# A one-layer decoder step on one core: feature tiles 4 and 5 as a stage of their own, and elementwise work in a fixed order by weight quarter

## The chip, the core and the metric

The kernel runs on one core of a Trainium2 chip. The time is the device time of that core from the start to the end of one execution, in microseconds (us). TensorE is called PE in the rows of the profile, and its weight loads PEld; VectorE is DVE, ScalarE is ACT, GpSimd is POOL, and SyncE, which issues the transfers, is SP.

## The reference, cut to what matters

One layer computes, for 256 prompt tokens and 8 x 4 sample tokens together (288 columns):

```
mod = silu(c) @ w_ada + b_ada            # six modulation vectors
h   = rms(x, g_mix) * (1 + sc_m) + sh_m
...                                      # two mixers, merged
x   = x + gt_m * (merged @ w_out)
h2  = rms(x, g_ffn) * (1 + sc_f) + sh_f
gate, up = split(h2 @ w_ffn_in)          # 2048 -> 2 x 5632
x   = x + gt_f * ((silu(gate) * up) @ w_ffn_out)
y   = rms(x, g_final)
```

The change touches the start of the FFN: the line that makes `h2` and the first columns of `h2 @ w_ffn_in`.

## The kernel before

Everything is held with features on the 128 partitions and tokens along the free axis: `x` is 16 feature tiles of 128 x 288. A product of a weight tile (128 x 128) and an activation tile (128 x 288) is made with three matmuls: both operands are split into a rounded high part and the rest, the low part, and high x high, high x low and low x high are added in PSUM (lines 501 to 503). So every weight tile that arrives costs two elementwise instructions besides the matmuls: ACT casts it to `hi`, DVE subtracts to `lo`. They are made for four 128 x 128 tiles at a time, 128 x 512 elements, called a quarter here, since a 1 MB block of weights has four of them. `Blk.high` and `Blk.low` make one quarter. Four `hi` and four `lo` buffers turn (`SPB = 4`), so a quarter's cast waits until PE is through with the quarter four before it.

The stream of weights is read in blocks of 1 MB by transfers on SP, five blocks ahead (`RAW = 5`). The main loop at the end of `_body` walks through `steps`: it issues the load of the block five steps on, splits blocks up to one ahead of the one that runs, and runs the step. A step of class `Do` is a piece of elementwise work. Where the wrapper `Pinned` has `on` set, the instructions of VectorE or ScalarE keep the order in which the code names them; with `on = None`, as from the `wD` blocks on, the scheduler may place them by its own priorities.

The output columns of `w_ffn_in` are grouped in 128-wide feature tiles, gate and up in turn: tiles 0 and 1 are the first gate and its up, 2 and 3 the second. The first four tiles are the stage `fk`. Their product needs `h2`, which needs the sum of squares of the whole finished `x`. To have PE busy meanwhile, `fk` multiplies the unnormalised `xg = x * gm2` (`scaled`, 298 columns: 288 tokens and the nine shift vectors and one of zeros), k by k, four output tiles side by side in four PSUM banks; `sink_fk` multiplies by the row factor `rb2` and adds the shift afterwards. Four blocks of four k each, each k with 12 matmuls.

Between these matmuls the row factor is made. `rstd2` runs behind matmul group (1, 1) of the first block: DVE adds the last square to the accumulator (`acc<-acc,t`), PE sums over partitions with a column of ones (three matmuls `px<-ones,acc`), DVE scales (`r<-px`), POOL takes the power -1/2 (`r<-r,mhalf`). `norm2` behind group (2, 2) spreads it: three matmuls `px<-ident,r`, an ACT copy `rb<-px`. Then `modulate` makes the 16 tiles of `h2`, in three pieces between the blocks of `fk`: for each k a DVE product `s<-x,rb`, an ACT affine step `t<-s,mod,gm`, two small POOL steps for the sample columns, an ACT cast `s<-t` (high part) and a DVE subtraction `s<-t,s` (low part).

Behind `fk` come the blocks `fi`, one feature tile each with all 16 k one after another (48 matmuls of 288 columns), from tile 4 on. A quarter of such a block holds four k. The 18 tiles 4 to 21 are woven with 16 steps of the last modulation product (`a5`), then the rest of the FFN follows in four parts. At the end of block 3 of `fk` all four of its PSUM banks are drained by `sink_fk` at once; `sink_fi` then joins gate and up.

Of the kernel before, what the change touches and what calls it, by code (L numbers as in the profile page):

```python
# [57 lines left out]
    "fk": (0, 4, 4),  # L58
    "fi": (0, 16, 1),
# [21 lines left out]
def _body(tc, nc, d, pc, pw, pslot, ptmp, pps):  # L81
# [150 lines left out]
    def turn(t, n=T):  # L232
        return t[:, :n].rearrange("p (a b) -> p b a", a=2)
# [308 lines left out]
    class KBlk(Blk):  # L542
        def run(self):
            if self.idx == 0:
                S["kps"] = [psmain() if j else psmisc() for j in range(self.nm)]
            nb = 16 // self.nk
            for k in range(self.nk):
                ah, al = (turn(t, TU) for t in self.rhs(self.idx * self.nk + k))
                first, last = self.idx + k == 0, self.idx == nb - 1 and k == self.nk - 1
                for j in range(self.nm):  # L550
                    ps = S["kps"][j]
                    wh, wl = self.parts[k * self.nm + j]
                    PE.matmul(ps[:, :TU], wh, ah, start=first, stop=False)  # L553
                    PE.matmul(ps[:, :TU], wh, al, start=False, stop=False)  # L554
                    self.last = PE.matmul(ps[:, :TU], wl, ah, start=False, stop=last)  # L555
                    for f in self.then.get((k, j), ()):
                        f()
            if self.idx == nb - 1:
                for j, ps in enumerate(S.pop("kps")):
                    self.sink(j, ps)  # L560
# [326 lines left out]
    def mk_h2(k0, k1):  # L887
        def f():
            modulate(range(k0, k1), lambda k: normed(k, S["rb2"]), gm2, 48, h2)

        return Do(f)


    act = {}

    def sink_fi(i, ps):
        f, up = i // 2, i % 2
        if not up:
            S["gate"] = ps
            return  # L900
        pg = S.pop("gate")
# [254 lines left out]
    def ffin(q):  # L1156
        fi = [Blk("fi", i - 4, h2.__getitem__, lambda j, ps: sink_fi(j + 4, ps)) for i in range(max(4, 22 * q), 22 * q + 22)]
        return fi
# [4 lines left out]
    fk = [KBlk("fk", i, xg.__getitem__, sink_fk) for i in range(4)]  # L1163
    fk[0].defer = fk[1].defer = True
    fk[0].then = {(1, 1): [rstd2], (2, 2): [norm2]}
    steps += [Do(fk[0].split), fk[0], Do(lambda: fk[1].split()), mk_h2(0, 6), fk[1], mk_h2(6, 11), fk[2], mk_h2(11, 16), fk[3]]
    a5 = ada("a5")
    steps += weave(ffin(0), [eight(a5[:8]), eight(a5[8:])], 0, 17)
# [175 lines left out]
```

## Time and profile before

| | us |
|---|---|
| runs shown | 1523.9, 1524.02, 1525.62 (median 1524.02) |
| the profiled execution, device time | 1523.81 |
| span of its instructions | 1521.9 |
| PE busy (share of the span) | 1511.2 (99%) |
| DVE busy | 994.1 (65%) |
| ACT busy | 742.4 (49%) |
| POOL busy | 135.4 (9%) |

The profiled execution is 0.2 us under the median; some 1.9 us of it lie before the first and after the last instruction. A row of the timeline has the start in us from the start of the span, the duration, engine, source line, operation, what is written and read, shapes, and in brackets how long the engine had been idle and what ended that. Matmuls are pipelined: one lasts 0.29 us, and the next starts 0.12 us after it; so a stall of PE is read from the distance of two starts, and seldom shows as idle time.

### The profile page before, as it was taken

Reading aid. Unit: us, or ns where it says so; the run is one execution under the profiler, and the core shown is the slowest. Engines: PE = TensorE matmul, PEld = TensorE weight load, DVE = VectorE, ACT = ScalarE, POOL = GpSimd, SP = SyncE. Lnnn points to the kernel's source line nnn. Section 1 sums busy time; section 2 is a strip of 40 time slices with the busy share of each in tenths; the row PEclk is TensorE's granted clock in tenths of the full one; section 3 lists DMA queues with packets and bytes.
Section 4 is the critical chain, followed back from the end, with each engine's and each line's share of the span. In section 5 each row is a group of like instructions: output and inputs, shape, how many; then the busy total and the mean of one; then the engine's idle time right before and its main releaser. Section 6 shows DMA issues by size and latency. Waiting matters only on the chain.

```text
span 1521.9 us, 31756 instructions
## 1 busy us (share of the span) xinstructions
PE 1511.2 (99%) x12596; PEld 1447.6 (95%) x12596; DVE 994.1 (65%) x2003; ACT 742.4 (49%) x1375; POOL 135.4 (9%) x272
## 2 busy tenths in 40 slices
PE   9999999999999999999999999999999999999997
PEld 7898999999899998989999899999999999999997
DVE  5886778978756666657954466555665556655575
ACT  5443454744445444447744444444444444444465
POOL 2554410000100000012300000000000000000000
PEclk9999999999999999999999999999999999999999
DMA  9877875777877788775599656554565545655452
GB/s 378 342 288 300 355 267 188 278 272 281 299 298 291 287 274 306 258 260 176 173 311 337 218 180 223 169 191 135 180 215 189 170 159 167 218 176 179 141 182 88
DMA packets 74436, 357.70 MB, mean 235 GB/s; under 512 B 8384, under 2 KB 28640, under 8 KB 44080
## 3 DMA queue, kind: packets, MB, share of 16 engines
q1 hardware_dynamic: 73792, 354.88, 65.6%
q8 instruction: 98, 1.61, 0.4%
q0 software_dynamic: 352, 0.73, 0.1%
q14 instruction: 50, 0.41, 0.1%
q10 hardware_dynamic: 144, 0.07, 0.0%
HBM read 352.56 MB, written 3.09 MB: 234 GB/s over the span
## 4 chain that ended last, share of the span: by engine, by line
PE 98%; DMA 1%; ACT 0%; DVE 0%; issue 0%; SPq 0%; DVEq 0%; POOL 0%; POOLq 0%
PE pm L501 30%; PE pm L503 30%; PE pm L502 30%; PE ada L383 6%; PE px L267 1%; DMA raw<-in_aB 1%; DMA raw<-in_aA 0%; PE pm L553 0%; PE pm L554 0%; PE pm L555 0%; PE pm L537 0%; PE px L595 0%; PE pm L267 0%; PE px L553 0%; PE px L554 0%; PE px L555 0%
## 5 line engine op out<-in xcount | busy, mean ns | idle before, releaser
L501 PE MATMUL pm<-s,hi 128*128 128x288 f32 (+1 forms) x3704 | 1063.3, 287 | 0.1
L503 PE MATMUL pm<-s,lo 128*128 128x288 f32 (+1 forms) x3704 | 1059.7, 286 | 0.2 <-DVE lo L115 0.2
L502 PE MATMUL pm<-s,hi 128*128 128x288 f32 (+1 forms) x3704 | 1059.5, 286 | 0.0
L115 DVE TENSOR_TENSOR lo<-raw,hi 128x512 fp32r<-128x512 f32 (+2 forms) x967 | 667.3, 693 | 404.3 <-ACT hi L115 390.6
L115 ACT CAST hi<-raw 128x512 fp32r<-128x512 f32 (+2 forms) x964 | 583.1, 606 | 663.3 <-PE pm L502 590.8
L501 PEld LDWEIGHTS pm<-s,hi 128*128 128x128 f32 x3704 | 700.0, 189 | 12.3 <-issue 10.2
L503 PEld LDWEIGHTS pm<-s,lo 128*128 128x128 f32 x3704 | 700.1, 189 | 0.4 <-DVE lo L115 0.4
L502 PEld LDWEIGHTS pm<-s,hi 128*128 128x128 f32 x3704 | 700.1, 189 | 0.0
L383 PE MATMUL ada<-raw,cs 128*32 128x512 f32 (+3 forms) x768 | 75.3, 525 | 1.7 <-DMA raw<-in_aB 0.9
L976 POOL TENSOR_TENSOR r<-r,mhalf 128x3 f32<-128x3 f32 x1 | 0.9, 863 | 768.4 <-DVE r L115 768.4
L115 DVE TENSOR_TENSOR s<-pm,s 128x288 f32<-128x288 f32 x128 | 57.5, 454 | 16.9 <-PE pm L503 16.5
L115 ACT CAST s<-t 128x288 fp32r<-128x288 f32 (+2 forms) x109 | 50.5, 465 | 24.1 <-DVE t L115 21.9
L383 PEld LDWEIGHTS ada<-raw,cs 128*32 128x32 f32 x768 | 21.7, 109 | 36.7 <-issue 27.4
L115 DVE TENSOR_TENSOR s<-t,s 128x288 fp32r<-128x288 f32 (+1 forms) x109 | 50.3, 463 | 7.9 <-ACT s L115 7.5
L115 DVE SCALAR_TENSOR_TENSOR t<-t,pm 128x288 f32<-128x288 f32 x84 | 37.9, 451 | 11.2 <-PE pm L503 11.2
L115 DVE SCALAR_TENSOR_TENSOR x<-pm,mod,x 128x256 f32<-128x256 f32 (+1 forms) x81 | 38.2, 472 | 2.4 <-PE pm L503 2.4
L278 POOL TENSOR_TENSOR t<-x,gm 128x32 f32<-128x32 f32 x16 | 7.9, 491 | 250.3 <-DVE acc L115 237.9
L665 POOL TENSOR_TENSOR s<-s,rb 128x288 f32<-128x288 f32 x30 | 29.6, 1009 | 0.0
L115 DVE SCALAR_TENSOR_TENSOR s<-pm,s 128x288 f32<-128x288 f32 x48 | 24.3, 510 | 0.0
L115 ACT ACTIVATE t<-x 128x288 f32<-128x288 f32 (+2 forms) x32 | 13.7, 428 | 19.2 <-DVE x L115 19.2
L666 POOL TENSOR_TENSOR s<-s 128x32 f32<-128x32 f32 x48 | 22.6, 484 | 0.0
L115 DVE TENSOR_TENSOR acc<-acc,t 128x288 f32<-128x288 f32 x36 | 16.4, 455 | 8.7 <-ACT t L115 8.7
(147 smaller groups left out, 558.5 us busy)
## 6 DMA issues: line engine op xcount, KB each, us to landing
raw<-in_fi SPq DMA_DIRECT2D x84, 1024.0 KB, 4.9
raw<-in_a SPq DMA_DIRECT2D x48, 1024.0 KB, 4.9
raw<-in_f SPq DMA_DIRECT2D x64, 704.0 KB, 4.1
raw<-in_wD SPq DMA_DIRECT2D x36, 1024.0 KB, 8.5
raw<-in_wC SPq DMA_DIRECT2D x20, 896.0 KB, 6.4
raw<-in_aE SPq DMA_DIRECT2D x16, 1024.0 KB, 6.8
s<-in_a SPq DMA_DIRECT2D x128, 128.0 KB, 5.3
raw<-in_wo SPq DMA_DIRECT2D x16, 1024.0 KB, 6.1
```

Of the source, the lines that this page charges most:

```text
L115: i = f(*args, **kw)
L267: return in_order(op(*args, **kw))
L278: G.tensor_tensor(sam(a[:, TP:T]), sam(x[:, k, TP:]), bc4(gm[:, k, 1:]), ALU.mult)
L383: PE.matmul(acc[32 * j : 32 * j + 32, c], cs[:, kt, :], self.raw[2 * j + h] if self.apart else self.raw[:, o : o + w], start=(kt < ks), st ...
L501: PE.matmul(ps[:, : self.n], wh, ah, start=first, stop=False)
L502: PE.matmul(ps[:, : self.n], wh, al, start=False, stop=False)
L503: self.last = in_order(PE.matmul(ps[:, : self.n], wl, ah, start=False, stop=last))
L665: G.tensor_tensor(a[:, :T], a[:, :T], S[rb], ALU.mult)
L666: G.tensor_tensor(sam(a[:, TP:T]), sam(a[:, TP:T]), bc4(a[:, T + 1 : T + NC]), ALU.add)
L976: G.tensor_tensor(r, r, mhalf, ALU.pow)
```

## The change

1. A new stage `fh` holds feature tiles 4 and 5: two blocks of eight k each, with the two tiles side by side as in `fk`, but on `h2` and with 288 columns. `KBlk` gets the number of columns as `n`, and keeps its PSUM banks in `held` until `release(j)` drains bank j. `fi` begins with tile 6.
2. `modulate` in three pieces is replaced by sixteen `Modulate` objects, and all elementwise work of the stage is ordered by hand. `pin(True)` sets the fixed order for V (VectorE) and A (ScalarE). `lead_in` splits three quarters; then `beat(g)`, at the start of the g-th quarter on PE (24 quarters: 16 of `fk`, 8 of `fh`), names in this order: the product of `h2` tile g - 3, the split of quarter g + 3, the affine step of tile g - 4, the split of tile g - 5. `KBlk.split` does nothing any more.
3. The four banks of `fk` are drained later: the first two behind groups (2, 1) and (6, 1) of the second `fh` block, the other two behind the first `fi` block, where the order is set free again. `sink_fi` keeps gates by number, as two may be open at once.
4. The weights of tiles 4 and 5 are packed by k on the host; the bytes that are read stay the same. `a5` is woven with 16 blocks in place of 18.

```diff
     "fk": (0, 4, 4),
+    "fh": (0, 8, 2),
...
     class KBlk(Blk):
+        held = None
+
+        def split(self):
+            pass
+
         def run(self):
+            n = self.n
             if self.idx == 0:
-                S["kps"] = [psmain() if j else psmisc() for j in range(self.nm)]
+                S["kps"] = [psmisc() if j == (n == T) else psmain() for j in range(self.nm)]
             nb = 16 // self.nk
             for k in range(self.nk):
-                ah, al = (turn(t, TU) for t in self.rhs(self.idx * self.nk + k))
+                ah, al = (turn(t, n) for t in self.rhs(self.idx * self.nk + k))
                 first, last = self.idx + k == 0, self.idx == nb - 1 and k == self.nk - 1
                 for j in range(self.nm):
                     ps = S["kps"][j]
                     wh, wl = self.parts[k * self.nm + j]
-                    PE.matmul(ps[:, :TU], wh, ah, start=first, stop=False)
-                    PE.matmul(ps[:, :TU], wh, al, start=False, stop=False)
-                    self.last = PE.matmul(ps[:, :TU], wl, ah, start=False, stop=last)
+                    PE.matmul(ps[:, :n], wh, ah, start=first, stop=False)
+                    PE.matmul(ps[:, :n], wh, al, start=False, stop=False)
+                    self.last = PE.matmul(ps[:, :n], wl, ah, start=False, stop=last)
                     for f in self.then.get((k, j), ()):
                         f()
             if self.idx == nb - 1:
-                for j, ps in enumerate(S.pop("kps")):
-                    self.sink(j, ps)
+                self.held = S.pop("kps")
+
+        def release(self, j):
+            self.sink(j, self.held[j])
...
     def sink_fi(i, ps):
         f, up = i // 2, i % 2
         if not up:
-            S["gate"] = ps
+            S["gate", f] = ps
             return
-        pg = S.pop("gate")
+        pg = S.pop(("gate", f))
...
     def ffin(q):
-        fi = [Blk("fi", i - 4, h2.__getitem__, lambda j, ps: sink_fi(j + 4, ps)) for i in range(max(4, 22 * q), 22 * q + 22)]
-        return fi
+        return [Blk("fi", i - 6, h2.__getitem__, lambda j, ps: sink_fi(j + 6, ps)) for i in range(max(6, 22 * q), 22 * q + 22)]
 
     def ffout(q):
         return [Blk(f"f{q}", i, act.__getitem__, sink_fo(q)) for i in range(16)]
 
-    fk = [KBlk("fk", i, xg.__getitem__, sink_fk) for i in range(4)]
-    fk[0].defer = fk[1].defer = True
+    fk = [KBlk("fk", i, xg.__getitem__, sink_fk, TU) for i in range(4)]
+    fh = [KBlk("fh", i, h2.__getitem__, lambda j, ps: sink_fi(j + 4, ps)) for i in range(2)]
+    fi0 = ffin(0)
+    m2 = [Modulate(k, gm2, 48, "rb2", h2) for k in range(16)]
+    quarters = [b for b in fk + fh for _ in range(4)] + [fi0[0]] * 3
+
+    def pin(on):
+        for e in (V, A):
+            e.on, e.last = on, None
+
+    def quarter(g):
+        if g < len(quarters):
+            quarters[g].high()
+            quarters[g].low()
+
+    def beat(g):
+        if 0 <= g - 3 < 16:
+            m2[g - 3].norm()
+        quarter(g + 3)
+        if 0 <= g - 4 < 16:
+            m2[g - 4].affine()
+        if 0 <= g - 5 < 16:
+            m2[g - 5].high()
+            m2[g - 5].low()
+
+    def lead_in():
+        pin(True)
+        for g in range(3):
+            quarter(g)
+
     fk[0].then = {(1, 1): [rstd2], (2, 2): [norm2]}
-    steps += [Do(fk[0].split), fk[0], Do(lambda: fk[1].split()), mk_h2(0, 6), fk[1], mk_h2(6, 11), fk[2], mk_h2(11, 16), fk[3]]
+    for g, b in enumerate(quarters[:24]):
+        b.then[(g % 4 if b in fk else g % 4 * 2), 0] = [lambda g=g: beat(g)]
+    fh[1].then[2, 1] = [lambda: fk[3].release(0)]
+    fh[1].then[6, 1] = [lambda: fk[3].release(1)]
+    fi0[0].defer = True
+    fi0[0].then = {0: [lambda: fk[3].release(2), lambda: fk[3].release(3), lambda: pin(None)]}
+    steps += [Do(lead_in), *fk, *fh, Do(lambda: [fh[1].release(j) for j in range(2)])]
     a5 = ada("a5")
-    steps += weave(ffin(0), [eight(a5[:8]), eight(a5[8:])], 0, 17)
+    steps += weave(fi0, [eight(a5[:8]), eight(a5[8:])], 0, 15)
```

The instructions are the same in number and kind on every engine. On SP two transfers of the new stage's weights stand where two of tiles 4 and 5 stood. The order on the other engines moves at the following places. `raw_9257`, `raw_9349` are the first two blocks of `fk`; the numbers of `px` and `pm` are PSUM banks.

**PE, the row factor.** In the program of before the column sums stand behind group (1, 1) of the first `fk` block:

```order
L553 MATMUL pm_9720<-s_9069,hi_9705 128x298
L554 MATMUL pm_9720<-s_9071,hi_9705 128x298
L555 MATMUL pm_9720<-s_9069,lo_9707 128x298
L267 MATMUL px_9743<-ones,acc_8358 128x1 x3
L553 MATMUL pm_9721<-s_9069,hi_9705 128x298
L554 MATMUL pm_9721<-s_9071,hi_9705 128x298
L555 MATMUL pm_9721<-s_9069,lo_9707 128x298
```

Fifteen matmuls, those up to group (2, 2), lie between this `px<-ones,acc` and the `px<-ident,r` of before. In the changed program:

```order
L560 MATMUL pm_9717<-s_9152,hi_9709 128x298
L561 MATMUL pm_9717<-s_9154,hi_9709 128x298
L562 MATMUL pm_9717<-s_9152,lo_9711 128x298
L268 MATMUL px_9747<-ones,acc_8358 128x1 x3
L560 MATMUL pm_9718<-s_9152,hi_9709 128x298
L561 MATMUL pm_9718<-s_9154,hi_9709 128x298
L562 MATMUL pm_9718<-s_9152,lo_9711 128x298
L560 MATMUL px_9715<-s_9161,hi_9722 128x298
L222 MATMUL px_9772<-ident,r_9745 128x128 x3
L561 MATMUL px_9715<-s_9163,hi_9722 128x298
L562 MATMUL px_9715<-s_9161,lo_9724 128x298
L560 MATMUL pm_9716<-s_9161,hi_9722 128x298
```

Here the sums stand 33 matmuls behind the start of `fk` in place of 18, and four matmuls separate them from the spreading of `r`, which now stands inside group (3, 0).

**DVE, at the same place.** Before, from the last residual addition on:

```order
L115 TENSOR_TENSOR lo_9715<-raw_9257,hi_9713 128x512
L115 TENSOR_TENSOR acc_8358<-acc_8358,t_9680 128x288
L115 TENSOR_TENSOR s_9690<-t_9683,s_9688 128x298
L115 TENSOR_SCALAR r_9741<-px_9743 128x3
L115 TENSOR_TENSOR lo_9787<-raw_9349,hi_9785 128x512
L115 TENSOR_TENSOR s_9699<-t_9692,s_9697 128x298
L115 TENSOR_TENSOR lo_9791<-raw_9349,hi_9789 128x512
```

And in the changed program:

```order
L116 TENSOR_TENSOR lo_9724<-raw_9257,hi_9722 128x512
L116 TENSOR_TENSOR s_9690<-t_9683,s_9688 128x298
L116 TENSOR_TENSOR lo_9740<-raw_9349,hi_9738 128x512
L116 TENSOR_TENSOR s_9699<-t_9692,s_9697 128x298
L116 TENSOR_TENSOR acc_8358<-acc_8358,t_9680 128x288
L116 TENSOR_SCALAR r_9745<-px_9747 128x3
L116 TENSOR_TENSOR lo_9764<-raw_9349,hi_9762 128x512
```

The addition `acc<-acc,t` stood ahead of the two `xg` subtractions (`s_9690`, `s_9699`) and of the first quarter of the second block (`lo` of `raw_9349`); it now stands behind these three.

**The end of the stage.** In the changed program `raw_9799` is the first `fi` block (tile 6), `px_9715` and `pm_9716` are the first two banks of `fk`, `pm_10115` and `px_10116` those of `fh`. ACT:

```order
L116 CAST hi_10280<-raw_9799 128x512
L116 CAST hi_10296<-raw_9799 128x512
L116 COPY w_1988_10303<-pm_9716 128x9
L116 ACTIVATE t_10309<-s_10267 128x288
L116 CAST s_10313<-t_10309 128x288
L116 ACTIVATE t_10323<-pm_10115 128x288
L116 CAST s_10327<-t_10323 128x288
L116 CAST hi_10333<-raw_9799 128x512
```

DVE:

```order
L116 TENSOR_TENSOR lo_10282<-raw_9799,hi_10280 128x512
L116 TENSOR_TENSOR lo_10298<-raw_9799,hi_10296 128x512
L116 TENSOR_TENSOR s_10305<-pm_9716,rb_9776 128x288
L116 TENSOR_SCALAR s_10305<-s_10305,w_1988_10303 128x256
L116 TENSOR_TENSOR s_10305<-s_10305,w_1988_10303 128x32
L116 SCALAR_TENSOR_TENSOR t_10309<-t_10309,s_10267 128x288
L116 SCALAR_TENSOR_TENSOR t_10309<-t_10309,s_10305 128x288
L116 TENSOR_TENSOR s_10315<-t_10309,s_10313 128x288
L116 SCALAR_TENSOR_TENSOR t_10323<-t_10323,pm_10115 128x288
L116 SCALAR_TENSOR_TENSOR t_10323<-t_10323,px_10116 128x288
L116 TENSOR_TENSOR s_10329<-t_10323,s_10327 128x288
L116 TENSOR_TENSOR lo_10335<-raw_9799,hi_10333 128x512
```

The split of the first `fi` block's last quarter (`hi_10333`, `lo_10335`) stands behind the drains of two `fk` banks and both `fh` banks. Before, the corresponding block had its four quarters split, and the drains of the four `fk` banks came after them.

More of the change, by code (lines that the diff above doesn't have):

```diff
@@ L885, in norm2 @@
         A.copy(S["rb2"], ps)
[L887 to L891, printed above, removed]
     act = {}
@@ L1310 @@
     arr["fk"] = np.ascontiguousarray(fk).reshape(4, P, 16 * P)
-    src["fi"] = src["fi"][:, 4 * P :]
+    fh = src["fi"][:, 4 * P : 6 * P].reshape(2, 8, P, 2 * P).transpose(0, 2, 1, 3)
+    arr["fh"] = np.ascontiguousarray(fh).reshape(2, P, 16 * P)
+    src["fi"] = src["fi"][:, 6 * P :]
     for name, (k0, nk, nmt) in STREAMS.items():
-        if name != "fk":
+        if name not in ("fk", "fh"):
             arr[name] = _pack(src[name], k0, nk, nmt)
```

## The prediction

> **What bounds the kernel now.** I read the page first: it says which engine is full, and so where a gain could lie at all.
>
> ```profile
> PE 1511.2 (99%) x12596; PEld 1447.6 (95%) x12596; DVE 994.1 (65%) x2003; ACT 742.4 (49%) x1375; POOL 135.4 (9%) x272
> ```
>
> PE is busy for 1511.2 of 1521.9 us, and the change leaves it the same matmuls. Only time in which PE stands still can be won or lost. But the ends of matmuls are modelled, so I read standing still from the distance of starts. Second view, the timeline of PE where `fk` ends and the block of tile 4 begins:
>
> ```profile
> 738.26 0.35 PE L555 MATMUL px<-s,lo 128*128 128x298 f32 x1
> 738.45 0.29 PE L553 MATMUL pm<-s,hi 128*128 128x298 f32 x1
> ...
> 740.86 0.29 PE L554 MATMUL pm<-s,hi 128*128 128x298 f32 x1
> 740.99 0.29 PE L555 MATMUL pm<-s,lo 128*128 128x298 f32 x1
> 741.11 0.29 PE L501 MATMUL pm<-s,hi 128*128 128x288 f32 x1
> 741.23 0.29 PE L502 MATMUL pm<-s,hi 128*128 128x288 f32 x1
> ...
> 743.81 0.29 PE L502 MATMUL pm<-s,hi 128*128 128x288 f32 x1
> 743.93 0.29 PE L503 MATMUL pm<-s,lo 128*128 128x288 f32 x1
> 744.15 0.39 PE L501 MATMUL pm<-s,hi 128*128 128x288 f32 x1
> 744.38 0.29 PE L502 MATMUL pm<-s,hi 128*128 128x288 f32 x1
> 744.88 0.39 PE L503 MATMUL pm<-s,lo 128*128 128x288 f32 x1 [0.21 <-DVE lo L115]
> 745.11 0.29 PE L501 MATMUL pm<-s,hi 128*128 128x288 f32 x1
> ```
>
> The undisturbed step is 0.123 us at 288 columns and 0.127 us at 298. From 743.93 to 745.11 four steps took 1.18 us in place of 0.49: 0.69 us lost, because the third quarter of tile 4's weights came late from DVE. Third view, the stretches: from 721.5 to 744.1 us, where `h2` is made beside `fk`, DVE and ACT are nearly full, and behind it they are not.
>
> ```profile
> core 0: us, PE busy (x) PEld busy (x) DVE busy (x) ACT busy (x) POOL busy (x), PEclk, DMA share, GB/s
> 721.50:744.10 22.60, 22.60 (x180) 22.48 (x178) 20.96 (x44) 21.22 (x47) 13.16 (x32) 1.00 0.41 141
> 756.00:770.00 14.00, 14.00 (x117) 14.00 (x116) 8.52 (x15) 6.63 (x13) 0.00 (x0) 1.00 0.86 277
> ```
>
> The step from 738.26 to 738.45 lost another 0.06; I found no other between 721 us and the end of tile 5. So at most 0.75 us can be won, 0.05% of the time.
>
> **The change part by part.** *Removed: the 0.69 us.* `h2` and the weights of tiles 4 and 5 get 96 matmuls (11.8 us) to be consumed in, k by k, where tile 4 alone asked for all sixteen k in 5.9 us. Per quarter of PE's work (12 matmuls, 1.52 us in `fk`, 1.47 in `fh`) a beat gives DVE one `lo`, one product and one subtraction, ACT one cast of weights, one affine step and one cast.
>
> ```profile
> 725.98 0.72 DVE L115 TENSOR_TENSOR lo<-raw,hi 128x512 fp32r<-128x512 f32 x1
> 726.63 0.49 DVE L115 TENSOR_TENSOR s<-t,s 128x288 fp32r<-128x288 f32 x1
> 727.05 0.49 DVE L115 TENSOR_TENSOR s<-x,rb 128x288 f32<-128x288 f32 x1
> 727.46 0.45 DVE L115 TENSOR_TENSOR s<-t,s 128x288 fp32r<-128x288 f32 x1
> ```
>
> Back to back these three take DVE 727.46 - 725.98 = 1.48 us: just the beat. Quarter g + 3 is split in beat g, so it has about two beats in hand, and `h2` tile k, done in beat k + 5, is first read in beat 16 + k/2. I take this stage as free of stalls; if that cover is gone, the price is that of the third rival. Gain: 0.75 us with the small step.
>
> *Added, first: the column sums wait for `acc`.* The timelines of DVE and ACT at the last `xg` tiles:
>
> ```profile
> 716.79 0.50 DVE L115 TENSOR_TENSOR acc<-acc,t 128x288 f32<-128x288 f32 x1
> 717.94 0.47 DVE L115 TENSOR_TENSOR s<-t,s 128x298 fp32r<-128x298 f32 x1 [0.65 <-ACT s L115]
> 718.43 0.16 DVE L115 TENSOR_SCALAR r<-px 128x3 f32<-128x3 f32 x1
> 718.51 0.69 DVE L115 TENSOR_TENSOR lo<-raw,hi 128x512 fp32r<-128x512 f32 x1
> 719.12 0.46 DVE L115 TENSOR_TENSOR s<-t,s 128x298 fp32r<-128x298 f32 x1
> 718.33 0.47 ACT L115 CAST s<-t 128x298 fp32r<-128x298 f32 x1
> ```
>
> The addition ran at 716.79; now it stands behind the two subtractions and the `lo`, whose times are set by ACT's casts, which keep their order. The second subtraction begins at 719.12 as before, and the next instruction some 0.36 us later: 719.48, plus 0.50, so `acc` is there at 719.98 and seen by PE near 720.0. PE begins `fk` at 715.39 and comes to the sums after 33 matmuls: 715.39 + 33 x 0.127 = 719.57. **Wait: 0.4 us.**
>
> *Added, second: the spreading waits for the power.* The rows of PE and POOL:
>
> ```profile
> 715.39 0.29 PE L553 MATMUL px<-s,hi 128*128 128x298 f32 x1
> 717.67 0.72 PE L267 MATMUL px<-ones,acc 128*128 128x1 f32 x6
> 718.26 0.37 PE L553 MATMUL pm<-s,hi 128*128 128x298 f32 x1
> 718.67 1.28 POOL L215 TENSOR_TENSOR r<-r,mhalf 128x3 f32<-128x3 f32 x1 [1.30 <-DVE r L115]
> 720.24 0.83 PE L221 MATMUL px<-ident,r 128*128 128x128 f32 x6
> ```
>
> From the start of the sums to the end of the power it takes 718.67 + 1.28 - 717.67 = 2.28 us, with the signal to PE about 2.33. Before, fifteen matmuls filled it (717.67 to 720.24 is 2.57 us, so 0.24 to spare). Now four matmuls do: 0.59 for the sums (718.26 - 717.67) and 4 x 0.127 make 1.10. **Wait: 1.2 us.** All matmuls of PE are queued behind it, none of which needs `r`. The two waits put `rb` about 2 us later on the clock, but PE is later by 1.6 too. The bound below is the power at 0.86 us, as it runs elsewhere:
>
> ```profile
> 1511.52 0.86 POOL L976 TENSOR_TENSOR r<-r,mhalf 128x3 f32<-128x3 f32 x1 [768.44 <-DVE r L115]
> ```
>
> That would be 0.8; I take 1.2, since line 215's own row is the nearest. With `acc` up to 0.3 later or earlier the first wait is 0.1 to 0.7.
>
> *Added, third: a PSUM bank for tile 6.* The first `fi` block writes the bank of `pm_9716`, which DVE drains behind `lo` of quarter 26, whose cast waits for the buffer of quarter 22. So from the moment PE has left quarter 22, 12 matmuls before the end of `fh`:
>
> ```profile
> 758.10 0.62 ACT L115 CAST hi<-raw 128x512 fp32r<-128x512 f32 x1 [0.85 <-PE pm L502]
> 758.75 0.69 DVE L115 TENSOR_TENSOR lo<-raw,hi 128x512 fp32r<-128x512 f32 x1 [0.78 <-ACT hi L115]
> 745.35 0.45 DVE L115 TENSOR_TENSOR s<-px,rb 128x288 f32<-128x288 f32 x1
> 745.71 0.45 DVE L115 TENSOR_TENSOR s<-pm,rb 128x288 f32<-128x288 f32 x1
> ```
>
> 0.1 from PE to the cast, 0.65 from cast to `lo`, 0.6 to the next DVE instruction (718.51 to 719.12 above), 0.45 for the drain, 0.05 to PE (both signals are estimates of mine): 1.85 us against 1.47 of matmuls. **Wait: 0.4 us.** It is read from distances only; between 0 and 0.7.
>
> *Added, fourth: the last quarter of tile 6.* Its split stands behind a chain in fixed order: two small DVE steps and four joining steps on DVE, three ACT steps among them, then cast and `lo`. With 0.36 to 0.5 us for each dependent step of 288 columns, 0.45 for the small ones, and 0.65 + 0.69 + 0.05 for the pair above, that is about 5.0 us from the start of tile 6 (0.45 + two joins 1.0, two ACT steps 0.9, two joins 1.0, one cast 0.4, 1.3 for the pair). PE asks for this `lo` after 38 matmuls, 38 x 0.123 = 4.7 us. **Wait: 0.3 us**, with the refill of the weights (0.1, as in the step 744.15 to 744.38) 0.4; between 0 and 1.
>
> *Moved at no cost:* the weights keep their bytes and arrive in 1 MB pieces as before, with the transfer engines at 0.41 in this stretch; the later joins of tiles 0 to 3 are wanted only by the second half of the FFN's product, tens of us on; `a5` moves by a block, and its matmuls are the same.
>
> The sum against the profiled execution: -0.75 + 0.4 + 1.2 + 0.4 + 0.4 = +1.65, and a small refill at the third wait, 0.1: 1523.81 + 1.75 = 1525.6 us. The median of the runs is 0.2 above that execution, so 1525.8. With all lower bounds (-0.75 + 0.1 + 0.8) it is +0.15, with all upper ones (0 + 0.7 + 1.3 + 0.8 + 1.1) +3.9.
>
> **The rivals.** *First: the late quarter goes and nothing comes for it*, -0.75: 1523.3 us. For it: waits read from distances may come out shorter, and the power has been seen at 0.86. Against it: even 0.86 us does not fit behind four matmuls of 0.51 together, and every later matmul stands behind the one that waits.
>
> *Second: the old stall stays as well.* If DVE is still behind by the time of tile 6, its quarters come late as tile 4's did, 0.69 again: 1526.5 us. For it: the drains of `fk` are DVE work, some 2 us per pair, and they now fall between tiles 5 and 6. Against it: behind 756 us DVE is busy for 8.52 of 14.0.
>
> *Third, on the other side: the beat does not hold, and PE runs at DVE's pace.* The groups of that stretch, durations end to end:
>
> ```profile
> L115 DVE TENSOR_TENSOR lo<-raw,hi 128x512 fp32r<-128x512 f32 x12 | 8.5, 716 | 0.9 <-ACT hi L115 0.9
> L115 DVE TENSOR_TENSOR s<-t,s 128x288 fp32r<-128x288 f32 x16 | 7.5, 473 | 0.7 <-ACT s L115 0.5
> L115 DVE TENSOR_TENSOR s<-x,rb 128x288 f32<-128x288 f32 x16 | 7.4, 478 | 1.0 <-ACT rb L115 1.0
> L312 POOL TENSOR_TENSOR t<-t,mod 128x32 f32<-128x32 f32 x16 | 6.3, 394 | 1.3
> ```
>
> 0.716 + 0.473 + 0.478 = 1.67 us a beat, if nothing overlaps; with a wait of 0.15 for ACT in the fixed order 1.82. Over the 16 beats with `h2` work that is 16 x (1.82 - 1.5) = 5.1 us late, of which two beats, 3.0, are in hand: 2.1 us more than forecast, 1527.9 us. It decides from 1.5 + 3.0/16 = 1.69 us a beat. Against it: the rows at 725.98 show 1.48 with POOL at work (13.16 of 22.6 us).
>
> [...] Its chance, 0.03, is part of the third rival's.
>
> **How the numbers follow.** Forecast 1525.8 us: 0.68. First rival 0.08, second 0.12, third 0.09; 0.03 for what I have not seen. The forecast, the second rival and the first all lie within 0.2% of 1524.02, which is 3.05 us and about what a measurement of this kernel can tell from no change: same 0.87. Slower by more needs the third rival or most upper bounds: 0.11. Faster by more is not to be had, with 0.75 us to win: 0.02. The range, 1524.0 to 1527.8, reaches from about the lower bounds to the upper ones; the runs before spread over 1.7 us by themselves.
>
> **What would show it.** Right: in the changed profile a PE wait of about 0.4 us on DVE's `acc` before `px<-ones`, one of about 1.2 us on POOL's `r` before `px<-ident`, even steps of 0.127 and 0.123 us from there to the end of `fh`, and steps of some 0.5 us at the start and in the last quarter of the first `fi` block. Wrong: no wait at `px<-ident`, so the power would have to end sooner than its row says; repeated waits on `lo` once per beat (third rival); or a change of time where the orders are the same.

## The result and the profile after

| | changed | before, on the same chip |
|---|---|---|
| median of 22 runs, us | 1526.55 | 1524.34 |
| lowest to highest, us | 1525.52 to 1528.64 | 1523.88 to 1525.67 |
| the profiled execution, us | 1526.3 | 1523.81 |
| span of its instructions, us | 1524.4 | 1521.9 |

The ratio is 1.0017, with a 95% interval of 1.0011 to 1.0023: 2.2 us slower, where 1.8 us was forecast. That is inside the 3.05 us called no change, though the interval leaves 1 out. The runs spread 1.7 times as far as before, 3.1 us against 1.8.

First the page's line of busy times of the changed kernel: the same matmuls, and every other engine about as busy as before.

```profile
PE 1512.4 (99%) x12596; PEld 1447.6 (95%) x12596; DVE 994.9 (65%) x2003; ACT 743.0 (49%) x1375; POOL 138.1 (9%) x272
```

PE's timeline in the first block of `fk`, around the row factor:

```profile
720.12 0.29 PE L562 MATMUL pm<-s,lo 128*128 128x298 f32 x1
720.63 0.83 PE L268 MATMUL px<-ones,acc 128*128 128x1 f32 x6 [0.22 <-DVE acc L116]
721.32 0.37 PE L560 MATMUL pm<-s,hi 128*128 128x298 f32 x1
...
721.79 0.29 PE L560 MATMUL px<-s,hi 128*128 128x298 f32 x1
723.06 0.93 PE L222 MATMUL px<-ident,r 128*128 128x128 f32 x6 [0.98 <-POOL r L216]
723.75 0.37 PE L561 MATMUL px<-s,hi 128*128 128x298 f32 x1
```

Subtract the undisturbed step of 0.127 us from each distance of starts. The column sums come 0.51 - 0.13 = 0.38 us late, for `acc`; the spreading comes 1.27 - 0.13 = 1.14 us late, for the power. The brackets show less (0.22 and 0.98), since they count from the modelled end of the matmul ahead. The same place on DVE and POOL:

```profile
719.75 0.46 DVE L116 TENSOR_TENSOR s<-t,s 128x298 fp32r<-128x298 f32 x1
720.13 0.45 DVE L116 TENSOR_TENSOR acc<-acc,t 128x288 f32<-128x288 f32 x1
721.50 0.16 DVE L116 TENSOR_SCALAR r<-px 128x3 f32<-128x3 f32 x1 [0.92 <-PE px L268]
721.74 1.26 POOL L216 TENSOR_TENSOR r<-r,mhalf 128x3 f32<-128x3 f32 x1 [3.92 <-DVE r L116]
```

The addition ends at 720.58 and PE starts the sums 0.05 us later; the power ends at 723.00 and PE starts the spreading 0.06 us later. The small matmuls behind each wait take 0.10 us longer than before (0.69 in place of 0.59 us to the next matmul of `fk`, both times). From there on the steps are even, 0.127 and then 0.123 us, to the end of `fh`. PE's timeline at the start and in the last quarter of tile 6:

```profile
755.10 0.29 PE L562 MATMUL px<-s,lo 128*128 128x288 f32 x1
755.69 0.36 PE L502 MATMUL pm<-s,hi 128*128 128x288 f32 x1 [0.30 <-DVE s L116]
755.89 0.29 PE L503 MATMUL pm<-s,hi 128*128 128x288 f32 x1
...
760.30 0.29 PE L503 MATMUL pm<-s,hi 128*128 128x288 f32 x1
760.60 0.39 PE L504 MATMUL pm<-s,lo 128*128 128x288 f32 x1
760.83 0.29 PE L502 MATMUL pm<-s,hi 128*128 128x288 f32 x1
```

The first step is 0.59 us and the next 0.20, together 0.54 too long; the later pair is 0.30 and 0.23, together 0.28 too long. The chain ahead of the first, on ACT and DVE:

```profile
753.83 0.62 ACT L116 CAST hi<-raw 128x512 fp32r<-128x512 f32 x1 [0.85 <-PE px L561]
754.49 0.69 DVE L116 TENSOR_TENSOR lo<-raw,hi 128x512 fp32r<-128x512 f32 x1 [0.78 <-ACT hi L116]
755.09 0.45 DVE L116 TENSOR_TENSOR s<-pm,rb 128x288 f32<-128x288 f32 x1
```

Cast, `lo`, drain, PE: the chain of the prediction, with the drain ending at 755.54 and PE at 755.69.

The whole account can be taken from the first matmul of `fk` to the end of the span. Before it is 1521.9 - 715.39 = 806.5 us; in the changed kernel `fk` starts at 716.07, and 1524.4 - 716.07 = 808.3. The stage thus costs 1.8 us. The other 0.7 us of the difference between these two executions lies ahead of `fk`, where the two programs do the same work. In the profiles of all runs below `fk` starts between 715.30 and 717.07 us; two of them that keep the order of before have 715.61 and 716.30. So 0.7 us there is no more than executions differ by. It does not explain a spread that is wider than before's.

### The profile page after: what moved, and what is told of

The parts are those of the page before. It is cut to its first block, busy times and chain, and to the rows that moved or that the text cites. A ratio compares the mean times of both kernels' runs of the same rounds, so it can differ in the third digit from the quotient of the medians.

```text
span 1524.4 us, 31753 instructions
## 1 busy us (share of the span) xinstructions
PE 1512.4 (99%) x12596; PEld 1447.6 (95%) x12596; DVE 994.9 (65%) x2003; ACT 743.0 (49%) x1375; POOL 138.1 (9%) x272
## 4 chain that ended last, share of the span: by engine, by line
PE 97%; DMA 2%; DVE 0%; ACT 0%; issue 0%; POOL 0%; SPq 0%; DVEq 0%; ACTq 0%
PE pm L502 30%; PE pm L504 29%; PE pm L503 29%; PE ada L384 5%; PE px L268 1%; DMA raw<-in_aB 1%; DMA raw<-in_aC 1%; PE pm L560 0%; PE pm L562 0%; PE pm L561 0%; DMA raw<-in_aA 0%; PE px L561 0%; PE pm L538 0%; PE px L560 0%; PE px L562 0%; DVE lo L116 0%
```

## The experiments

Each ran beside the kernel before on the same chip. The kernel before had medians of 1524.29 to 1524.36 us over 18 to 33 runs, so an experiment's median is to be held against those and against the changed kernel's 1526.55. A median of eleven runs also moves with the time at which `fk` starts, so the time from the first matmul of `fk` to the end of the span is given too, for the profiled execution: 806.5 us before, 808.3 in the changed kernel. Diffs are shown in part, and against the changed kernel except where said.

**1. The changed kernel once more (again).** No edit.

> The changed kernel once more. Its profile showed the stage 1.7 us longer, but the medians differ by 2.2 us, and its 22 runs spread over 3.1 us where those of before spread over 1.8. Theory: the stage costs 1.6 to 1.8 us in every execution (waits of 0.4, 1.15, 0.5 and 0.3 us against 0.75 removed), and the rest comes from waits for transfers in the first 150 us, which differ from run to run. Then this profile shows the same four waits to 0.1 us, while PE reaches the first matmul of fk at another time than 716.2. Rival: the waits in the stage themselves vary by half a us and more.

Measured: 1526.84 us (1525.38 to 1528.88, 11 runs); the ratio is 1.0014 [1.0005, 1.0023]. The four waits are there with the same lengths. But the profiled execution, 1528.41 us, shows something more behind the second. PE's timeline:

```profile
720.57 0.29 PE L562 MATMUL pm<-s,lo 128*128 128x298 f32 x1
721.08 0.83 PE L268 MATMUL px<-ones,acc 128*128 128x1 f32 x6 [0.22 <-DVE acc L116]
...
722.23 0.29 PE L560 MATMUL px<-s,hi 128*128 128x298 f32 x1
723.50 1.26 PE L222 MATMUL px<-ident,r 128*128 128x128 f32 x6 [0.98 <-POOL r L216]
...
725.06 0.46 PE L560 MATMUL pm<-s,hi 128*128 128x298 f32 x1
725.31 0.46 PE L561 MATMUL pm<-s,hi 128*128 128x298 f32 x1
```

Nothing is waited for here, and yet the steps are 0.25 us, twice the normal. The stretches of the same execution, with the granted clock in the third column from the end:

```profile
723.75:724.00 0.25, 0.25 (x4) 0.25 (x4) 0.00 (x0) 0.00 (x0) 0.00 (x0) 0.91 0.00 0
724.00:727.25 3.25, 3.25 (x15) 3.25 (x15) 1.57 (x3) 0.92 (x2) 1.33 (x3) 0.50 0.02 5
727.25:727.50 0.25, 0.25 (x4) 0.25 (x3) 0.00 (x0) 0.21 (x1) 0.23 (x1) 0.77 0.00 0
1522.50:1522.75 0.25, 0.00 (x0) 0.00 (x0) 0.00 (x0) 0.00 (x0) 0.00 (x0) 0.84 1.12 438
```

The granted clock is halved. If it changes once within a stretch, a mean of 0.91 puts the fall at 723.75 + 0.25 x 0.41/0.5 = 723.955, and a mean of 0.77 the return at 727.25 + 0.25 x 0.23/0.5 = 727.365: 3.41 us at half clock. (The last row is used below.) Here the stretch from `fk` to the end takes 1526.5 - 716.52 = 810.0 us, 1.7 more than in the profile above. Half of 3.41 us is 1.7. So the expectation that the stage costs 1.6 to 1.8 us in every execution was wrong, and so was its rival, since the waits did not change.

**2 and 3. Two more looks at the changed kernel (look1, look2).** No edit.

> The changed kernel, one more profile, to see where an execution of it loses more than the waits. Theory: where the execution is over 1526.8 us, a stretch of steps of 0.248 us behind the wait for the power, as in one of the two profiles so far. Rival: the third wait, before tile 6, is followed by such a stretch as well.

> The same once more, with the same expectations: 0.248 us steps behind the wait for the power in an execution over 1526.8 us and none in one under it; by the rival, such steps behind the wait before tile 6.

Measured: 1528.98 and 1526.42 us, beside 1524.04 before. Look 1 has the half clock, at the same place and for 3.41 us; look 2 hasn't. From `fk` to the end they take 810.0 and 808.3 us: the two values already seen. So two of four profiled executions paid 1.7 us more, and nothing seen but the clock tells them apart. No fall was seen behind the waits of tile 6.

**4. The spreading a row of matmul groups later (spread_later).** The spreading goes behind group (3, 3), and the `h2` work one beat later with it.

```diff
-        if 0 <= g - 3 < 16:
-            m2[g - 3].norm()
+        if 0 <= g - 4 < 16:
+            m2[g - 4].norm()
         quarter(g + 3)
-        if 0 <= g - 4 < 16:
-            m2[g - 4].affine()
+        if 0 <= g - 5 < 16:
+            m2[g - 5].affine()
...
-    fk[0].then = {(1, 1): [rstd2], (2, 2): [norm2]}
+    fk[0].then = {(1, 1): [rstd2], (3, 3): [norm2]}
```

> The changed kernel with the spreading of the row factor at group (3, 3) in place of (2, 2), and the work on h2 one beat later. Eighteen matmuls and more then lie between the sums and the spreading. Theory (the second wait is the 2.3 us from sums to power, not covered by four matmuls): no wait at px<-ident, the other three as they were, 1.1 us faster than the changed kernel, so 1.1 us over before. Rival (the wait moves on with rb, since h2 comes a beat later): under 0.5 us faster, with new waits at the start of fh.

Measured: 1524.7 us (1524.25 to 1526.65, 11 runs), ratio 1.0003 [0.9995, 1.0012]. PE's timeline shows the spreading start one step behind the matmul ahead of it, with no bracket:

```profile
722.61 0.29 PE L562 MATMUL pm<-s,lo 128*128 128x298 f32 x1
722.73 0.83 PE L222 MATMUL px<-ident,r 128*128 128x128 f32 x6
```

The other three waits stay (0.38, 0.54 and 0.28 as before). From `fk` to the end it takes 807.1 us, 1.2 less than in the changed kernel without a fall: the wait and the 0.1 us behind it, and the 1.1 us expected. The median is 1.9 us lower, which is more than the wait itself. No fall of the clock is in the profile; that the other executions had none either was not seen.

**5. PE kept busy across the second wait (fill).** Eight products of a constant, not used for anything, stand ahead of the spreading, and four matmuls of `fk` that stood ahead of it now stand behind.

```diff
     def norm2():
+        ps = psmisc()
         with behind(fk[0].last):
-            ps = rstd_bcast(S["r2"])
+            for _ in range(8):
+                i = PE.matmul(ps[:, 384:512], ones, ones, start=True, stop=True)
+        with behind(i):
+            ps = rstd_bcast(S["r2"], ps)
...
```

> The changed kernel with eight idle-time matmuls of ones ahead of the spreading of the row factor; the four matmuls that stood there come after it. PE then works from the sums to the spreading, instead of standing still for 1.15 us, but is through with fk no sooner: the same steps are 0.5 us longer by distance. Theory (a profile of the changed kernel showed steps of 0.248 us and a granted clock of 0.52 from 724 to 727.5 us; the clock falls in some executions because PE stood still before): no step of 0.248 us, spread of the runs under 1.5 us, median 1525.8 to 1526.2, so under the changed kernel's 1526.6 although the work is longer. Rival (the slow executions have another cause): the spread stays near 3 us, and the median is 1527.

Measured: 1526.66 us (1525.98 to 1527.14, 11 runs), ratio 1.0014 [1.0005, 1.0023]. The rows of PE:

```profile
720.88 0.83 PE L268 MATMUL px<-ones,acc 128*128 128x1 f32 x6 [0.22 <-DVE acc L116]
721.57 2.03 PE L894 MATMUL px<-ones 128*128 128x128 f32 x16
723.44 0.83 PE L222 MATMUL px<-ident,r 128*128 128x128 f32 x6
```

The spread fell from 3.5 us (in run 1) to 1.2 and the clock stays at 1.00 in the profile, as the clock theory wants. The median did not come down, 0.5 us above the upper end expected. The rows say why: from the sums to the first matmul of `fk` behind the spreading, PE takes 3.15 us here (to 724.03) with none of `fk`'s matmuls in between, and 3.12 in the changed kernel (720.63 to 723.75) with four. These four, 0.5 us, are paid again: 808.9 us from `fk` to the end.

**6. The power taken twice (power_twice).** A second POOL step raises `r` to the power of one, so only the wait grows.

```diff
         G.tensor_tensor(r, r, mhalf, ALU.pow)
+        if n == D:
+            G.tensor_tensor(r, r, ones[:, 0:3], ALU.pow)
```

> The changed kernel with a second power (exponent 1) on POOL behind the first, so that PE waits some 2.5 us before the spreading in place of 1.15. Theory of the clock: the fall comes in every execution, or nearly; 1.3 us for the longer wait and 0.8 to 1.7 us for the clock against the changed kernel's median, 1528.5 to 1529.5. Rival (chance falls of the clock that have nothing to do with the wait): 1.3 us, 1527.9, with the same share of slow executions.

Measured: 1528.4 us (1527.38 to 1530.01, 6 runs), ratio 1.003 [1.0018, 1.0041]. The timeline of POOL and PE, and below it a stretch of the same execution:

```profile
722.47 0.85 POOL L218 TENSOR_TENSOR r<-r,ones 128x3 f32<-128x3 f32 x1
...
723.37 0.94 PE L224 MATMUL px<-ident,r 128*128 128x128 f32 x6 [1.91 <-POOL r L218]
```

```profile
724.25:724.50 0.25, 0.25 (x4) 0.25 (x3) 0.00 (x0) 0.15 (x1) 0.00 (x0) 0.60 0.00 0
```

The wait is 0.93 us longer (2.07 us), but the median 1.9 us higher than the changed kernel's, 0.1 under the range of the theory and 0.5 over the rival's figure. The clock falls in the profile, and the stretch from `fk` takes 810.9 us: the changed kernel's 808.3, the longer wait and 1.7. Five of six runs lie at 1528.3 us or above, so the fall seems to have become the rule; that is read from their times.

**7. The addition ahead of the three quarters (acc_early).** The last addition to `acc` is named before the fixed order begins.

```diff
...
-        if not fill:
+        if not fill and not added:
             V.tensor_tensor(ss.acc, ss.acc, ss.last, ALU.add)
...
-        S["r2"] = token_rstd3(S["acc2"], D)
+        S["r2"] = token_rstd3(S["acc2"], D, added=True)
...
     def lead_in():
+        ss = S["acc2"]
+        V.tensor_tensor(ss.acc, ss.acc, ss.last, ALU.add)
         pin(True)
```

> The changed kernel with the last addition to the sum of squares named ahead of the first three quarters, so that the column sums stand behind group (1, 1) again. The scaling of r on DVE still stands behind lo of the second block and the last xg subtraction, at about 719.5 us. Theory: the first wait goes, and one of 0.8 to 0.9 us stays before px<-ident: 0.7 to 0.8 us faster than the changed kernel in executions without the fall of the clock. Rival (only the first wait goes): 0.4 us.

Measured: 1524.46 us (1524.04 to 1525.44, 11 runs), ratio 1.0002 [0.9993, 1.001]. The first wait is gone and the second is 0.38 us. The timeline of POOL and PE:

```profile
719.59 0.89 POOL L216 TENSOR_TENSOR r<-r,mhalf 128x3 f32<-128x3 f32 x1 [2.30 <-DVE r L116]
...
720.53 0.93 PE L222 MATMUL px<-ident,r 128*128 128x128 f32 x6 [0.21 <-POOL r L216]
```

Moving one instruction gives back 2.1 us in the median, and 1.2 us from `fk` to the end (807.1). More than the first wait went: with `acc` ready early the sums run in their place, and fifteen matmuls of `fk` stand between them and the spreading in place of four. The wait that stays is half of the 0.8 to 0.9 us expected; the power took 0.89 us here in place of 1.26.

**8. The end of the stage in another order (tail_order).** The second bank of `fk` is drained one quarter earlier, and tile 6's last quarter is split ahead of the drains of `fh`.

```diff
-    quarters = [b for b in fk + fh for _ in range(4)] + [fi0[0]] * 3
+    quarters = [b for b in fk + fh for _ in range(4)] + [fi0[0]] * 4
...
-    fh[1].then[6, 1] = [lambda: fk[3].release(1)]
+    fh[1].then[4, 1] = [lambda: fk[3].release(1)]
...
-    steps += [Do(lead_in), *fk, *fh, Do(lambda: [fh[1].release(j) for j in range(2)])]
+    steps += [Do(lead_in), *fk, *fh, Do(lambda: (quarter(27), fh[1].release(0), fh[1].release(1)))]
```

> The changed kernel with the second fk bank drained behind group (4, 1) in place of (6, 1), and the last quarter of tile 6 split ahead of the drains of the two fh banks. Theory (third and fourth wait are orders of DVE and ACT, one instruction standing behind another): no wait in tile 6, 0.8 us faster than the changed kernel. Rival (DVE has too much to do there, whatever the order): a wait of 0.5 us or more appears in tile 6 or 7 instead.

Measured: 1525.13 us (1524.59 to 1527.16, 11 runs), ratio 1.0006 [0.9997, 1.0014]. Tile 6 runs without a wait; the first two stay, and so does a fall of the clock in the profiled execution (1526.69 us). From `fk` to the end it takes 809.2 us; without the 1.7 us of the fall that is 0.8 less than the changed kernel, as expected. The median is 1.4 lower.

**9. All three together (best).**

> The three repairs together: the addition named early, the spreading at group (3, 3) with h2 a beat later, and the two orders at the end of the stage. Theory: no wait of PE from 716 to 765 us, so the 0.75 us of the old kernel are won, 1523.6 us, and with no standing still no fall of the clock: a spread under 1.5 us. Rival (removing the waits here lets others come, from the beat that does not hold): 1524.3 or more.

Measured: 1523.55 us (1523.02 to 1525.22, 11 runs) against 1524.36; ratio 0.9997 [0.9988, 1.0006]. In the profile no wait of PE is left from the start of `fk` through tile 6, and this stretch takes 1522.0 - 716.29 = 805.7 us, 0.8 less than before. That is the whole of the old stall, and what the change could give at most. The median is that of the theory, and below both kernels; against the kernel before it can't be told from no change. The spread, 2.2 us, did not come under the 1.5 us expected.

**10. `fh` without the fixed order (fh_alone).** The elementwise work of the stage is left to the scheduler as in the kernel before; only tiles 4 and 5 as a stage remain.

```diff
-    for g, b in enumerate(quarters[:24]):
-        b.then[(g % 4 if b in fk else g % 4 * 2), 0] = [lambda g=g: beat(g)]
...
-    steps += [Do(lead_in), *fk, *fh, Do(lambda: [fh[1].release(j) for j in range(2)])]
+    steps += [Do(fk[0].split), fk[0], Do(lambda: fk[1].split()), mk_h2(0, 6), fk[1], mk_h2(6, 11), fk[2], mk_h2(11, 16), fk[3], *fh]
...
```

> The kernel before with the stage for tiles 4 and 5 alone: no fixed order, h2 made in three pieces, the fk banks drained at once behind fk. Theory of the prediction (the stall in tile 4 goes since tiles 4 and 5 consume h2 and weights over 11.8 us): the 0.69 us go, 1523.6 us. Rival (the third quarter's lo was late by DVE's backlog whatever PE reads it for): a stall of about 0.7 us stays in the third quarter of fh, 1524.3 us.

Measured: 1524.24 us (1523.77 to 1524.72, 11 runs) against 1524.29; ratio 0.9999 [0.999, 1.0008]. PE in the third quarter of `fh`:

```profile
744.17 0.29 PE L557 MATMUL px<-s,lo 128*128 128x288 f32 x1
744.40 0.39 PE L555 MATMUL pm<-s,hi 128*128 128x288 f32 x1
744.63 0.29 PE L556 MATMUL pm<-s,hi 128*128 128x288 f32 x1
745.13 0.39 PE L557 MATMUL pm<-s,lo 128*128 128x288 f32 x1 [0.21 <-DVE lo L116]
745.35 0.29 PE L555 MATMUL px<-s,hi 128*128 128x288 f32 x1
```

Four steps take 1.18 us: the old stall of 0.69 us, in its old place, again for a late `lo`. None of the four new waits is there, and from `fk` to the end it takes 806.5 us, as before. So the stage by itself makes no wait and cures nothing; the fixed order, with it, does both.

What stood ahead of that `lo` is in the timelines of ACT and DVE of the kernel before:

```profile
742.64 0.94 ACT L115 CAST s<-t 128x288 fp32r<-128x288 f32 x2
743.49 1.14 ACT L115 CAST hi<-raw 128x512 fp32r<-128x512 f32 x2
742.49 1.58 DVE L115 TENSOR_TENSOR s<-t,s 128x288 fp32r<-128x288 f32 x3
744.13 1.29 DVE L115 TENSOR_TENSOR lo<-raw,hi 128x512 fp32r<-128x512 f32 x2
```

Both engines do `h2` work first: ACT casts two tiles of it before it begins the quarter's `hi` at 743.49, and DVE is through with three subtractions at 744.07. `lo` begins as both `hi` (0.6 us a cast) and the subtractions end. In the changed kernel the `lo` of the same quarter is done at 743.5 us, and PE comes to it near 746.4, 24 matmuls behind the start of `fh` at 743.47.

**11. One more DVE product in each beat (beat_plus).** Its result is not used.

```diff
             m2[g - 3].norm()
+            V.tensor_tensor(S["extra"][:, :T], x[:, g - 3, :], S["rb2"], ALU.mult)
...
```

> The changed kernel with one more DVE product of 288 columns in each of the sixteen beats that make h2; its result is not used. It takes 0.36 to 0.42 us, so DVE's beat is about 1.85 us against 1.5 of PE. Theory (two beats in hand, 3.0 us): 16 x 0.35 - 3.0 = 2.6 us over the changed kernel, as stalls on lo in fh. Rival (DVE's beat has room that the durations hide): under 1 us over it, at the end of fh alone.

Measured: 1528.66 us (1527.55 to 1530.02, 8 runs), ratio 1.003 [1.0019, 1.004]: 2.1 us over the changed kernel, where the formula of the third rival gives 2.6. PE:

```profile
752.32 0.29 PE L561 MATMUL pm<-s,hi 128*128 128x288 f32 x1
752.67 0.39 PE L562 MATMUL pm<-s,lo 128*128 128x288 f32 x1
...
756.82 0.29 PE L562 MATMUL px<-s,lo 128*128 128x288 f32 x1
758.15 0.36 PE L502 MATMUL pm<-s,hi 128*128 128x288 f32 x1 [1.04 <-DVE s L116]
```

The step from 752.32 is 0.35 us; the same comes in four successive beats of `fh`, at 746.91, 748.71, 750.52 and 752.32, and the wait at tile 6's bank has grown from 0.47 to 1.21 us. These late steps are 1.80 us apart, where a quarter takes PE 1.47. So with one more product DVE is the bound. Without it none of these steps was seen, so the changed kernel's beat holds, with less than one product to spare.

**12. Only the host's packing (layout).** The kernel before, with the weights of tiles 4 and 5 in a tensor of their own.

```diff
+    "fh": (0, 16, 1),
...
-            SY.dma_start(self.raw[:, a:b], d[self.name][self.idx][:, a:b])
+            src = d[self.name][self.idx] if self.name != "fi" else d["fh"][self.idx] if self.idx < 2 else d["fi"][self.idx - 2]
+            SY.dma_start(self.raw[:, a:b], src[:, a:b])
...
```

> The kernel before, unchanged but that the weights of tiles 4 and 5 lie in a tensor of their own, as in the changed kernel; every instruction as before. Theory (the 0.5 us that the stage does not explain come from where the weights lie in memory): 0.4 to 0.8 us slower than before, with a wider spread. Rival (they come from the draw of runs and chips): within 0.2 us of before, with its spread. The 0.69 us in the third quarter of tile 4 stay in both.

Measured: 1524.37 us (1523.88 to 1525.32, 11 runs), ratio 1.0001 [0.9992, 1.001]. Another tensor in memory costs nothing that can be told here, and the old stall stays.

**When the clock falls.** The profiles that the runs left answer this without a further run. In run 1 the granted clock also falls when PE is through: the row 1522.50:1522.75 puts that at 1522.50 + 0.25 x 0.34/0.5 = 1522.67. From the fall at 723.955 to there it is 798.72 us. The fall itself lasts 3.41 us, and 798.72/3.41 is 234.2; with 234 whole steps, one is 3.4133 us. Read in the same way, the fall lasts from 724.69 to 728.10 us in look 1, from 722.985 to 726.395 in tail_order and from 724.30 to 727.715 in power_twice, so 3.41 us in each. If the clock is decided on a grid of 3.4133 us, the end of any execution gives its grid; the grid is an estimate from these falls. For the changed kernel's first profile:

```profile
1520.50:1520.75 0.25, 0.00 (x0) 0.00 (x0) 0.00 (x0) 0.00 (x0) 0.00 (x0) 0.58 1.04 410
```

The fall is at 1520.54; 234 grid steps back is 721.82, one more 718.41. The same was done for each profile that had both waits; a wait is counted from one step behind the start of the last matmul.

| execution | PE stands still, us | the grid, us | longest standstill in one window, us | with the sums, us | clock halved |
|---|---|---|---|---|---|
| changed, first profile | 720.25–720.63, 721.92–723.06 | 718.41, 721.82, 725.24 | 1.14 | 1.14 | no |
| look 2 | 720.39–720.76, 722.05–723.19 | 717.43, 720.84, 724.26 | 1.14 | 1.75 | no |
| beat_plus | 720.60–720.98, 722.26–723.40 | 718.86, 722.27, 725.68 | 1.13 | 1.13 | no |
| again | 720.70–721.08, 722.36–723.50 | 720.54, 723.95 | 1.52 | 2.21 | from 723.95 |
| look 1 | 721.25–721.63, 722.92–724.06 | 721.28, 724.69 | 1.49 | 2.19 | from 724.69 |
| tail_order | 719.82–720.21, 721.49–722.63 | 719.57, 722.98 | 1.53 | 2.21 | from 722.98 |
| power_twice | 719.65–720.02, 721.30–723.37 | 720.89, 724.30 | 2.07 | 2.07 | from 724.30 |
| beat_plus, its end | from 1519.11 on | 1517.57, 1520.99, 1524.40 | 1.88 | 1.88 | not at 1520.99 |

In the three executions without a fall in the stage the grid parts the two waits. In the four with one, both waits share a window, or the long wait of power_twice lies in one. The 1.21 us at tile 6 in beat_plus lie wholly in one window (756.40 to 759.82) too, and no fall follows: the mean granted clock of that execution is 0.999, where a second fall beside that at its end would make it 0.998.

How much standing still it takes depends on whether the three `px<-ones,acc`, 0.69 us on one column each, count as work. The end of beat_plus tells, since PE's last matmul stands early in a window there:

```profile
1518.28 0.83 PE L268 MATMUL px<-ident,r 128*128 128x128 f32 x6
```

```profile
1524.25:1524.50 0.25, 0.00 (x0) 0.00 (x0) 0.00 (x0) 0.00 (x0) 0.00 (x0) 0.80 0.91 346
```

By the modelled end PE is through at 1519.11, and the clock falls at 1524.40. One grid step before that is 1520.99, where PE had stood still for at least 1.88 us of the window, and the clock did not fall. So the 1.49 to 1.53 us of the two waits can't be the whole of what counted, unless the end of an execution follows another rule. With the sums as standing still (the table's fifth column) the four windows before a fall have 2.07 to 2.21 us, and the others at most 1.88. By that reading, an estimate from these eight rows, the limit lies between 1.88 and 2.07 us of 3.41. The least that a fall followed is the 2.07 us of power_twice, a single wait. The grid stands differently to the program in each execution: in the table the sums start from 0.35 us (look 1) to 3.33 us (look 2) behind a grid point. So the same kernel can have both times.

The two waits of the changed kernel span 720.25 to 723.06, 2.81 us. If all phases of the grid are equally likely, both lie whole in one window in (3.41 - 2.81)/3.41 = 0.18 of them, an estimate. With the sums they are 2.21 us, so by the limits above 0.14 to 0.33 us may be cut off at either end, which makes it 0.26 to 0.37. Of 35 executions of this kernel 14 took 1527.1 us or more; that these are the ones with the half clock is read from their times, except for the two profiled.

## Why the prediction was right or wrong

- **First wait, 0.4 us forecast for `acc`: 0.38.** The addition stood where the order put it, and acc_early removed the wait.
- **Second wait, 1.2 us for the power: 1.14.** POOL's row carried over (1.26 for 1.28 us). Moving the spreading removed it, taking the power twice made it 2.07. The signal to PE, estimated at 0.05 us, took 0.06 (723.00 to 723.06).
- **Third, 0.4 us and a refill of 0.1 at tile 6's bank: 0.47 and 0.07.** The two signals in that sum, 0.1 and 0.05 us, were my estimates; from the end of the drain to PE it was 0.15 (755.54 to 755.69). Fourth, 0.4 us in its last quarter: 0.28. Both went with tail_order.
- **Removed, 0.75 us: it went, but the reason was wrong.** The step "`h2` and the weights of tiles 4 and 5 get 96 matmuls (11.8 us) to be consumed in, k by k" put the cure on the stage. fh_alone has the stage and keeps the stall whole. With the stage it is the order by quarter that brings each `lo` in time; in the free order casts and subtractions for `h2` stand ahead of it. Whether the fixed order would do without `fh` was not tried.
- **The sum, +1.75 us against the profiled execution: the stage cost +1.8 there.** The measured terms close it: 0.38 + 1.14 + 0.54 + 0.28 - 0.75, and twice the 0.10 us behind the small matmuls, which the sum lacked, make 1.79. The profiled execution itself was 0.7 us above 1525.6, by the time at which PE reaches `fk`. The prediction named "a change of time where the orders are the same" as a sign of being wrong; 0.7 us is too little for one, as that time differs by 1.8 us over the profiles.
- **What failed is a term that the sum lacked:** "with all upper ones" the costs were added as if standing still cost its own length only. The granted clock stood in the rows quoted (1.00 in both stretches), and I took it as given. Where the two waits share a window, 1.7 us come on top. The mean over 22 runs, 1526.94 against 1524.42, is +2.5 us; 1.8 + (0.26 to 0.37) x 1.7 is 2.2 to 2.4. The median has little of it, since most runs seem to have none.
- **The rivals.** The first, that nothing replaces the stall, fell at the first timeline; best shows what it would have been, 0.8 us less in the stretch. The second fell: PE's steps are even up to tile 6. The third did not happen, but beat_plus shows its mechanism and about its price (2.1 us for 2.6) once each beat has one product more. The third would have shown as a late `lo` once per beat; the trace of the changed kernel has none. Of its chance, 0.03 was given to a cause that no run shows. What the rows show of POOL's work beside DVE's is that before the change the `lo` at 725.98 took 0.72 us with POOL busy, and the one at 758.75 took 0.69 with POOL idle.
- **The bounds.** The power at 0.86 us was no idle bound: 0.89 was seen in acc_early. Why it takes 1.26 us at one time and 0.89 at another stays open.

## What to carry to other kernels

When work is put in a fixed order, look for the small instruction that another engine waits for, and count the matmuls left between the two ends of its chain: here it takes 2.4 us from the start of the sums to the start of the spreading, and the new order left four matmuls, half a microsecond. On PE, when it is full, add up the standstills that fall within 3.41 us of each other, the smallest matmuls between them included: here, in three executions, the clock was halved behind 1.49 to 1.53 us of standing still together with 0.69 us of one-column matmuls; a run spread that grows with the change (here 1.7 times) is the sign to look at the granted clock in more than one profile. And test each half of a change alone: the half that was credited here did nothing by itself.

## What the runs showed of the hardware

In four executions (again, look 1, tail_order, power_twice) the granted clock of PE fell to 0.50 for 3.41 us, with steps of 0.25 us in place of 0.127; that costs 1.7 us (810.0 us from `fk` to the end in place of 808.3). In run 1 a further fall came at its end, 798.72 us later, 234 steps of 3.413 us; taken as a grid, it stands differently to the program in each execution, with a grid point 0.35 to 3.33 us ahead of the sums. The fall followed a window with 2.07 us of standing still, and three with 1.49 to 1.53 us of it and all or nearly all of 0.69 us of one-column matmuls. It did not follow windows with 1.13 to 1.21 us, nor one with 1.88 us at the end of an execution. Keeping PE busy with products that nobody reads kept the clock at 1.00 in the one profile of it (fill), and saved nothing: a median of 1526.66 us against 1526.55, and 808.9 us from `fk` to the end against 808.3 without a fall.

The POOL power on 128x3 took 1.26 us in the changed kernel and 0.89 us in acc_early; no run shows why.
